# Attention steps split into turn and value products, head pairs side by side, a reordered mixer and a delta-net norm summed by tokens

## The chip, the cores and the metric

The kernel runs on one core of one Trainium2 chip. The metric is the device time of one execution in microseconds (us), as the median of several runs. A core has a matrix engine (TensorE, PE in the rows), a vector engine (VectorE, DVE), a scalar engine (ScalarE, ACT), GpSimd (POOL) and a queue of transfers (SyncE, SP). Each takes its own instructions in order, and they wait for one another through semaphores. Products go into the banks of PSUM, from which VectorE and ScalarE copy them out.

## The reference

Two blocks work on 256 tokens of 1024 features, in float32. The first block has a convolution with a dense MLP, an attention with a forget gate, and a mixture of experts; the second has a mixer and an MLP. The change touches the forget attention and the mixer.

```python
def forgetting_attention(q, k, v, logf_cum):       # 16 heads of 64, causal
    ...
    s = jnp.einsum("bqhd,bkhd->bhqk", qf[:, q0:q1], kf[:, :q1]) * scale
    s = s + logf_cum[:, :, q0:q1, None] - logf_cum[:, :, None, :q1]
    ...
    p = jax.nn.softmax(s, axis=-1).astype(v.dtype)
    outs.append(jnp.einsum("bhqk,bkhd->bqhd", p, v[:, :q1]))

# the mixer: 8 heads of block attention, 8 heads of a gated delta net, on one projection
proj = jnp.einsum('bsd,dc->bsc', h, w_in[l])
o_att = moba_attention(att_q, att_k, att_v, rel_bias)          # 256 tokens: one causal block
o_gdn = gated_deltanet(gdn_qkv, gdn_z, gdn_a, gdn_b, ...)
mix = jnp.einsum('bsc,cd->bsd', jnp.concatenate([o_att, o_gdn], axis=-1), w_out[l])

# the delta net: convolution and SiLU, norm of q and k by heads, decays g, chunks of 64 tokens
g = -jnp.exp(A_log) * jax.nn.softplus(a + dt_bias)
uw = lax.linalg.triangular_solve(a_mat, rhs, left_side=True, lower=True, unit_diagonal=True)
...
o = o * lax.rsqrt(jnp.mean(o * o, axis=-1, keepdims=True) + EPS) * norm_w
o = o * jax.nn.silu(z)
```

## The kernel before

**Products and weights.** A float32 product by weights is made of three products of rounded parts: hi by hi, hi by lo and lo by hi. Each weight block comes by DMA (raw); ScalarE rounds it (whi) and VectorE takes the difference (wlo). A projection chunk is 256 columns wide and consists of 48 matmuls of 256 columns. Products of computed values (scores, value products, the deltanet's) are plain float32, of which each is two instructions in the trace.

**Order.** The program is written as Python that emits instructions; a scheduler sets the order on each engine, and tc.issue_after(x) keeps what follows behind x. last_pe[0] is the last matmul or transpose emitted by mm or transpose, so a block under tc.issue_after(last_pe[0]) stands behind it. In the mixer, seq(...) runs each of its steps in that way; in the forget attention the steps are emitted in the order of a string, without a pin.

**Forget attention (forget_block).** k_chunk, q_chunk and v_chunk project 256 columns each, that is four heads (banks pk, pq, pv). lin_small makes the 16 forget logits (bank psm), which VectorE brings to the buffer smo, two transposes (bank pf) turn, and softplus rows (sp_...) turn into gates; forget_gates sums them over the tokens (bank pc) into nlc, which each head's scores take in as a bias. For a pair of heads, att_scores makes biases and score products (bank sc) and the softmax; its two heads lie on rows 0 to 63 and 64 to 127 of the same operands. att_values transposes the probabilities (bank pt, three for each head), ScalarE copies them (pT), and the value products go to the two halves of the columns of one bank (po). In the string, s stands for the scores of a pair, o for values, and q, k, v for chunks.

**Mixer (mixer_block).** Projections of the block attention (paq for q and k, pav for v) and of the delta net (pqkv, six gdn_chunk; pz, two gate_chunk) stand in one sequence with the pairs of the attention. The delta net's small product gives a and b (psm, smo, transposes pab), from which softplus rows and gg make the decays; five products with a triangle of ones sum them up (pgc). gdn_chunk copies its bank to cpad and makes a convolution of eight rows on VectorE (qkv). After all chunks head_sums (pn) and a root, a reciprocal and a split in two parts (two_parts, buffer parts) give the norms of q and k, which normalize spreads over the heads by products (pbc). Then gdn_scores makes decays and scores for four pairs of heads (pdec, ps), v_tokens turns v (pvt), first_level and level solve the triangular systems by doubling (pi, pu, pm, pog), and out_rows makes pieces of the output projection (acc). At the end the delta net's output is squared (osq), summed by heads (bank pn of 8 rows, in the code pn2), and its norm is spread with two matmuls a bank (pob) and multiplied in, together with the gate zs.

Of the kernel before, what the change touches and what calls it, by code (L numbers as in the profile page):

```python
# [10 lines left out]
AF = mybir.ActivationFunctionType  # L11
# [3 lines left out]
P = 128  # L15
T = 256
# [86 lines left out]
def kernel(ctx: ExitStack, tc: tile.TileContext, ins: dict, out: bass.AP):  # L103
# [749 lines left out]
    def att_values(hp, probs, vtok, ohi, olo):  # L853

        po = bank("po", "acc")
        pTs = []
        for j in range(2):
            pt = bank("pt")
            for i in range(3):
                pe.transpose(pt[:, i * P:(i + 1) * P], probs[j][:, i * P:(i + 1) * P], ident)  # L860
            pT = wk("pT", 384)
            act.activation(pT, pt[:, :384], AF.Copy)
            pTs.append(pT)
        for j in range(2):
            s = slice(j * 64, (j + 1) * 64)
            vc = slice((2 * hp + j) * 64, (2 * hp + j + 1) * 64)
            mm(po[s, 0:T], vtok[0][:, vc], pTs[j][:, 0:T], True, False)
            mm(po[s, P:T], vtok[1][:, vc], pTs[j][:, T:384], False, True)
        split(ohi, olo, po[:, :T])


    def forget_block(x, feed, nxt):
# [16 lines left out]
        def forget_logits():  # L889
            fT = lin_small(ins["w_f"], 16, hkv, feed.R, -1.0)  # L890
# [28 lines left out]

        def values(hp):  # L920
            att_values(hp, pend.pop(hp), vt, oT[0][hp], oT[1][hp])
# [349 lines left out]
    def mixer_block(x, feed, nxt):  # L1271
# [68 lines left out]

        def att_out():
            h_, pr = pend.pop(0)
# [15 lines left out]
        qk_out(1, 0, first[1])  # L1358

# [3 lines left out]
        for tb in range(2):  # L1363
            pe.transpose(pab[:, tb * 16:(tb + 1) * 16], abT[:16, tb * P:(tb + 1) * P], ident[0:16, 0:16])
# [4 lines left out]
        act.activation(v3(beta, 8), pab3[:, :, 8:16], AF.Sigmoid)  # L1369
        gg = sm("gg", 16, bufs=1)  # L1370
# [8 lines left out]
        for tb in range(2):  # L1379
            mm(pg[:, tb * 8:(tb + 1) * 8], C("tri"), gg[:, tb * 8:(tb + 1) * 8], True, True)  # L1380
        mm(pg[:, 16:24], C("ones"), gg[:, 0:8], True, True)
        mm(pg[:8, 256:384], gg[:, 0:8], C("tri"), True, True)
        mm(pg[:8, 384:512], gg[:, 8:16], C("tri"), True, True)
# [23 lines left out]
        seq(lambda: gdn_chunk(4), lambda: gdn_chunk(5))  # L1407
# [3 lines left out]
        seq(head_sums)  # L1411
# [17 lines left out]
        seq(lambda: gate_chunk(0), normalize)  # L1429
# [151 lines left out]
        seq(v_tokens, lambda: gdn_scores(0), lambda: gate_chunk(1))  # L1581
# [276 lines left out]
```

## Time and profile before

| | us |
|---|---|
| Timed runs: median of 3 | 1704.89 (1704.25 to 1707.17) |
| Profiled execution | 1699.43 |
| its span in the trace | 1697.7 |
| TensorE busy in it | 1625.0 (96%) |
| VectorE busy | 1250.7 (74%) |
| ScalarE busy | 1016.9 (60%) |
| GpSimd busy | 78.9 (5%) |

The stages in the trace are: convolution and MLP until 323.5 us, forget attention to 449.1, experts to 1284.1, the mixer to 1503.9 and the last MLP to the end. The mixer's projections and block attention take 1302.9 to 1397.2, the scores of the delta net and its first levels until 1435.4, the later levels until 1485.8, the norm and the last pieces of the output projection until 1503.9. Busy shares are a mean over stages with different limits, so they don't say what a change in one stage is worth; the waits in that stage do.

### The profile page before, as it was taken

The page shows a single profiled execution, that of the slowest core. Times are in us where ns is not written, and L with a number is a line of the kernel's source. Part 1 is how long each engine was busy: PE and PEld are TensorE (multiplying, and loading weights), DVE is VectorE, ACT ScalarE, POOL GpSimd, SP SyncE. Part 2 cuts the span into 40 slices and gives each one's busy share as a digit, 9 for nine tenths or more (in the row PEclk, how much of TensorE's full clock was granted, in tenths as well). Part 3 has the DMA queues.
Part 4 walks back from the last instruction along what each step waited for, and adds up shares of the span by engine and source line. Part 5 has one row for each costly group of instructions (what it writes and reads, how often), then busy time and mean ns, then how long its engine had stood idle before and what let it go on. Part 6 is the DMA issues. An engine that isn't in the chain of part 4 may idle for free.

```text
span 1697.7 us, 26302 instructions
## 1 busy us (share of the span) xinstructions
PE 1625.0 (96%) x10450; PEld 1375.9 (81%) x10450; DVE 1250.7 (74%) x1738; ACT 1016.9 (60%) x1464; POOL 78.9 (5%) x113
## 2 busy tenths in 40 slices
PE   7999999999889999999999999999998988989998
PEld 6769999898778788777878778787777877879997
DVE  4466555676578998989988898989887775385554
ACT  4245444565467777777777777777676454354442
POOL 2400000000000000000000000000000000011111
PEclk9989999999899999999999999999999998999999
DMA  6655555435528889999999998899995341035551
GB/s 237 186 181 192 178 194 177 175 133 199 199 103 324 323 335 355 343 351 352 335 337 352 373 356 335 338 349 341 361 354 186 125 142 46 3 139 200 196 180 45
DMA packets 59973, 408.71 MB, mean 241 GB/s; under 512 B 7353, under 2 KB 7745, under 8 KB 12609
## 3 DMA queue, kind: packets, MB, share of 16 engines
q1 hardware_dynamic: 56448, 396.86, 63.4%
q0 software_dynamic: 3104, 9.55, 2.0%
q8 instruction: 85, 1.39, 0.3%
q10 hardware_dynamic: 288, 0.52, 0.1%
q14 instruction: 48, 0.39, 0.1%
HBM read 404.67 MB, written 2.24 MB: 240 GB/s over the span
## 4 chain that ended last, share of the span: by engine, by line
PE 60%; DVE 5%; ACT 3%; issue 2%; DMA 1%; POOL 0%; DVEq 0%; POOLq 0%; ACTq 0%
PE pgu L145 27%; PE acc L145 18%; PE pu L145 6%; DVE wlo L156 2%; PE pi L145 2%; PE paq L145 1%; ACT whi L167 1%; PE pqkv L145 1%; PE mpt L1178 1%; PE scat L145 1%; DMA raw<-in_moe_w_down_dram 1%; ACT xg L1058 0%; DVE qkv L159 0%; DVE Vi L156 0%; PE po L145 0%
## 5 line engine op out<-in xcount | busy, mean ns | idle before, releaser
L156 DVE TENSOR_TENSOR wlo<-raw,whi 128x1024 fp32r<-128x1024 f32 x752 | 890.8, 1222 | 254.7 <-ACT whi L167 246.8
L167 ACT ACTIVATE whi<-raw 128x1024 fp32r<-128x1024 f32 x752 | 761.1, 1057 | 256.0 <-PE pu L145 71.8
L145 PE MATMUL pgu<-whi,xg 128*128 128x512 f32 x1408 | 467.7, 398 | 5.9 <-DVEq L1106 4.1
L145 PEld LDWEIGHTS pgu<-whi,xg 128*128 128x128 f32 x1408 | 265.6, 189 | 63.2 <-PEq L1106 4.4
L145 PE MATMUL pgu<-wlo,xg 128*128 128x512 f32 x704 | 283.8, 403 | 1.1 <-issue 1.0
L145 PEld LDWEIGHTS pgu<-wlo,xg 128*128 128x128 f32 x704 | 132.9, 189 | 39.6 <-DVE wlo L156 13.2
L145 PE MATMUL acc<-wlo,mhi 128*128 128x512 f32 x352 | 135.1, 391 | 1.1 <-DVE wlo L156 1.1
L145 PE MATMUL acc<-whi,mlo 128*128 128x512 f32 x352 | 134.4, 389 | 0.0
L145 PE MATMUL acc<-whi,mhi 128*128 128x512 f32 x352 | 127.1, 390 | 1.4 <-ACT whi L167 1.4
L145 PE MATMUL pu<-hlo,whi 128*128 128x256 f32 x432 | 122.3, 283 | 0.5 <-DVE hlo L159 0.5
L145 PE MATMUL pu<-hhi,whi 128*128 128x256 f32 x432 | 122.2, 283 | 0.0
L145 PE MATMUL pu<-hhi,wlo 128*128 128x256 f32 x432 | 122.2, 283 | 0.0
L1072 ACT ACTIVATE msg<-pgu,rse 128x256 f32<-128x256 f32 x88 | 41.8, 475 | 81.1 <-PE pgu L145 81.1
L145 PE MATMUL acc<-wlo,fhi 128*128 128x512 f32 x216 | 85.1, 394 | 0.0
L145 PE MATMUL acc<-whi,fhi 128*128 128x512 f32 x216 | 85.0, 394 | 0.0
L145 PE MATMUL acc<-whi,flo 128*128 128x512 f32 x216 | 85.0, 394 | 0.0
L167 ACT ACTIVATE mhi<-mpt 128x256 fp32r<-128x256 f32 x88 | 33.9, 385 | 84.5 <-PE mpt L1178 84.5
L145 PEld LDWEIGHTS pu<-hlo,whi 128*128 128x128 f32 x432 | 82.7, 191 | 1.3 <-DVE hlo L159 0.7
L145 PEld LDWEIGHTS pu<-hhi,whi 128*128 128x128 f32 x432 | 82.6, 191 | 0.6
L145 PEld LDWEIGHTS pu<-hhi,wlo 128*128 128x128 f32 x432 | 82.7, 191 | 0.0
L145 PEld LDWEIGHTS acc<-wlo,mhi 128*128 128x128 f32 x352 | 66.1, 188 | 17.1 <-DVE wlo L156 3.3
L145 PEld LDWEIGHTS acc<-whi,mhi 128*128 128x128 f32 x352 | 65.9, 188 | 15.8 <-ACT whi L167 2.0
(400 smaller groups left out, 2640.8 us busy)
## 6 DMA issues: line engine op xcount, KB each, us to landing
raw<-in_moe_w_gu_dram SPq DMA_DIRECT2D x172, 1024.0 KB, 6.4
raw<-in_moe_w_down_dram SPq DMA_DIRECT2D x86, 1024.0 KB, 6.3
raw<-in_w_up_dram SPq DMA_DIRECT2D x16, 1024.0 KB, 4.8
raw<-in_w_down_dram SPq DMA_DIRECT2D x16, 1024.0 KB, 4.9
raw<-in_w_in_dram SPq DMA_DIRECT2D x14, 1024.0 KB, 4.8
raw<-in_ffn_w_gate_dram SPq DMA_DIRECT2D x11, 1024.0 KB, 4.9
raw<-in_ffn_w_up_dram SPq DMA_DIRECT2D x11, 1024.0 KB, 4.8
raw<-in_ffn_w_down_dram SPq DMA_DIRECT2D x11, 1024.0 KB, 4.8
```

The source lines that it names most:

```text
L145: last_pe[0] = pe.matmul(o, l, r, start=start, stop=stop, skip_group_check=True).ins
L156: return (eng or dve).tensor_tensor(out=o, in0=a, in1=b, op=op)
L167: return act.activation(hi, src, AF.Copy), tt(lo, src, f(hi), ALU.subtract, eng)
L1072: act.activation(sg, pgu[:, 0:256], AF.Silu, scale=r)
L1178: pe.transpose(pt[:, j * P:(j + 1) * P], p["sg"][:, j * P:(j + 1) * P], ident)
```

## The change

The scores of a pair get both banks ahead, and the two heads alternate instruction by instruction. att_values is split: att_turn makes the transposes and copies, att_values the products, with the two heads alternating. In the forget attention the string has a new letter t for the turn, each step is pinned behind the last matmul, the forget logits are transposed after v_chunk(0), and q_chunk(0) comes ahead of the gates. In the mixer the projections, the attention steps, gate_chunk(1), the decay products and the pieces of the output projection take other places. The delta net's norm is summed with the tokens on the partitions (16 small matmuls into a bank of 16 columns), so that root and reciprocal work on 128 by 16 elements, and it is spread with a broadcast as the stationary operand.

```diff
@@ att_scores, att_values
+        pss, rows = [bank("sc") for _ in range(2)], [slice(j * 64, (j + 1) * 64) for j in range(2)]
+        if add_bias:
+            for j in range(2):
+                add_bias(pss[j][:, 0:384], 2 * hp + j)
+        for j, s in enumerate(rows):
+            mm(pss[j][:, 0:P], qT[s, 0:P], kT[s, 0:P], not add_bias, True)
+        for j, s in enumerate(rows):
+            mm(pss[j][:, P:P + T], qT[s, P:T], kT[s, :], not add_bias, True)
         for j in range(2):
             h = 2 * hp + j
-            s = slice(j * 64, (j + 1) * 64)
-            ps_ = bank("sc")
-            if add_bias:
-                add_bias(ps_[:, 0:384], h)
-            mm(ps_[:, 0:P], qT[s, 0:P], kT[s, 0:P], not add_bias, True)
-            mm(ps_[:, P:P + T], qT[s, P:T], kT[s, :], not add_bias, True)
+            ps_ = pss[j]
...
+    def att_values(hp, pTs, vtok, ohi, olo):
+
+        po = bank("po", "acc")
+        for w in range(2):
+            for j in range(2):
+                s = slice(j * 64, (j + 1) * 64)
+                vc = slice((2 * hp + j) * 64, (2 * hp + j + 1) * 64)
+                mm(po[s, w * P:T], vtok[w][:, vc], pTs[j][:, w * T:T + w * P], w == 0, w == 1)
         split(ohi, olo, po[:, :T])
@@ forget_block
         k_chunk(0)
-        nls = forget_logits()
+        small = lin_small_mm(ins["w_f"], 16, hkv, feed.R, -1.0)
         v_chunk(0)
+        nls = forget_logits(small)
         feed.rest()
         k_chunk(1)
+        q_chunk(0)
         forget_gates(nls)
-        for step in "q0 s0 s1 q1 o0 v1 o1 s2 s3 k2 o2 q2 o3 v2 s4 s5 k3 o4 q3 o5 s6 s7 v3 o6 o7".split():
-            {"k": k_chunk, "q": q_chunk, "v": v_chunk, "s": scores, "o": values}[step[0]](int(step[1]))
+        steps = {"k": k_chunk, "q": q_chunk, "v": v_chunk, "s": scores, "t": turn, "o": values}
+        for step in ("v1 s0 s1 q1 t0 k2 o0 t1 s2 q2 o1 t2 s3 v2 o2 t3 s4 k3 o3 t4 s5 q3 o4 t5 s6 s7 v3 o5 t6 t7 o6 o7"
+                     .split()):
+            with tc.issue_after(last_pe[0]):
+                steps[step[0]](int(step[1]))
@@ mixer_block
+        seq(lambda: gdn_chunk(2))
+        x = feed.base()
...
+        seq(lambda: att_probs(0))
         gg = sm("gg", 16, bufs=1)
...
-        seq(lambda: gdn_chunk(2), lambda: att_probs(0), lambda: v_chunk(0))
-        x = feed.base()
+        seq(lambda: v_chunk(0), lambda: att_probs(1), lambda: gdn_chunk(3))
...
+        seq(decays)
...
-        seq(lambda: att_probs(1), lambda: gdn_chunk(3), att_out, lambda: qk_chunk(0, 1), att_out, lambda: qk_chunk(1, 1),
-            lambda: att_probs(2), lambda: gdn_chunk(0), lambda: att_probs(3), lambda: v_chunk(1), att_out,
-            lambda: gdn_chunk(1), att_out)
+        seq(att_t, lambda: qk_chunk(0, 1), att_out, att_t, lambda: qk_chunk(1, 1), att_out, lambda: gdn_chunk(0),
+            lambda: att_probs(2), lambda: gdn_chunk(1), lambda: att_probs(3), lambda: v_chunk(1), att_t)
...
-        seq(lambda: gdn_chunk(4), lambda: gdn_chunk(5))
+        seq(lambda: gdn_chunk(4), att_out, att_t, lambda: gdn_chunk(5))
...
-        seq(head_sums)
+        seq(att_out, head_sums)
...
-        seq(lambda: gate_chunk(0), normalize)
+        seq(lambda: gate_chunk(0), lambda: gate_chunk(1), normalize)
...
-        seq(v_tokens, lambda: gdn_scores(0), lambda: gate_chunk(1))
-        seq(lambda: gdn_scores(1), lambda: out_rows(0, 0), lambda: first_level(0), lambda: out_rows(1, 0),
-            lambda: gdn_scores(2), lambda: level(0, 2), lambda: out_rows(2, 0), lambda: gdn_scores(3))
+        seq(lambda: gdn_scores(0), v_tokens, lambda: out_rows(0, 0), lambda: gdn_scores(1), lambda: out_rows(1, 0),
+            lambda: out_rows(2, 0), lambda: first_level(0), lambda: gdn_scores(2), lambda: level(0, 2),
+            lambda: out_rows(3, 0), lambda: gdn_scores(3))
...
-        seq(lambda: out_rows(3, 0), lambda: level(0, 4), lambda: first_level(1))
+        seq(lambda: level(0, 4), lambda: first_level(1))
...
         def out_sums():
-            for b in range(4):
-                mm(pn2[:8, :T], v3(C("ind"), 16)[:, b, 0:8], osq[:, b * T:(b + 1) * T], b == 0, b == 3)
+            for tb in range(2):
+                for b in range(4):
+                    mm(pn2[:, tb * 8 + 2 * b:tb * 8 + 2 * b + 2], osq[:, b * T + tb * P:b * T + (tb + 1) * P],
+                       v3(C("ind"), 16)[:, 0, 0:2], True, True)
...
-        rn2 = two_parts(rn2, 8)
...
             for b in range(4):
-                mm(pbs[b // 2][:, b % 2 * T:(b % 2 + 1) * T], hsel[0:40, b * P:(b + 1) * P], rn2, True, True)
+                for tb in range(2):
+                    o = b % 2 * T + tb * P
+                    for j in range(2):
+                        c = tb * 8 + 2 * b + j
+                        mm(pbs[b // 2][j * 64:(j + 1) * 64, o:o + P], rn2[:, c:c + 1].to_broadcast([P, 64]), ident, True, True)
```

How the instructions stand now is shown at three places. First TensorE in the forget attention, at the first pair's value products before. Its six transposes and three pv matmuls stand just ahead of these rows, and v_chunk(1), whose matmuls 4 to 7 are the pv rows, goes on behind po.

```order
L145 MATMUL pv_3698<-whi_3701,hhi_3119 128x256
L145 MATMUL pv_3698<-wlo_3702,hhi_3119 128x256
L145 MATMUL pv_3698<-whi_3701,hlo_3121 128x256
L145 MATMUL po_3679<-pT_3684,v_3198 64x256
L145 MATMUL po_3679<-pT_3684,v_3199 64x128
L145 MATMUL po_3679<-pT_3690,v_3198 64x256
L145 MATMUL po_3679<-pT_3690,v_3199 64x128
L145 MATMUL pv_3698<-whi_3701,hhi_3119 128x256
```

And after the change: the end of a k chunk, the value products of pair 0, the turn of pair 1 and the scores of pair 2.

```order
L145 MATMUL pk_3752<-hhi_3120,wlo_3760 128x256
L145 MATMUL po_3812<-pT_3744,v_3198 64x256
L145 MATMUL po_3812<-pT_3750,v_3198 64x256
L145 MATMUL po_3812<-pT_3744,v_3199 64x128
L145 MATMUL po_3812<-pT_3750,v_3199 64x128
L148 MATMUL pt_3819<-cm,sc_3658 128x128 x3
L148 MATMUL pt_3825<-cm,sc_3669 128x128 x3
L145 MATMUL sc_3831<-nlc_3211,rsel 128x384
L145 MATMUL sc_3832<-nlc_3211,rsel 128x384
L145 MATMUL sc_3831<-kT_3200,qT_3202 128x128
L145 MATMUL sc_3832<-kT_3200,qT_3202 128x128
L145 MATMUL sc_3831<-kT_3200,qT_3202 128x256
```

The chunk between turn and products is whole now, and the rows of two heads alternate in po and sc. Second, TensorE in the mixer at the decay products: before, they stand behind v_chunk(0) and ahead of the scores of pair 1.

```order
L145 MATMUL pav_13192<-whi_13199,hhi_12809 128x256
L145 MATMUL pav_13192<-wlo_13200,hhi_12809 128x256
L145 MATMUL pav_13192<-whi_13199,hlo_12811 128x256
L145 MATMUL pgc_13255<-gg_13067,cm 128x8 x3
L145 MATMUL pgc_13255<-cm,gg_13067 8x128 x2
L145 MATMUL sc_13269<-ak_12881,aq_12880 128x128
L145 MATMUL sc_13269<-ak_12881,aq_12880 128x256
L145 MATMUL sc_13283<-ak_12881,aq_12880 128x128
L145 MATMUL sc_13283<-ak_12881,aq_12880 128x256
```

After the change they stand directly behind the last three matmuls of gdn_chunk(3).

```order
L145 MATMUL pqkv_13283<-hhi_12809,whi_13290 128x256
L145 MATMUL pqkv_13283<-hlo_12811,whi_13290 128x256
L145 MATMUL pqkv_13283<-hhi_12809,wlo_13291 128x256
L145 MATMUL pgc_13353<-gg_13167,cm 128x8 x3
L145 MATMUL pgc_13353<-cm,gg_13167 8x128 x2
L148 MATMUL pt_13367<-cm,sc_13145 128x128 x3
L148 MATMUL pt_13373<-cm,sc_13156 128x128 x3
L145 MATMUL paq_13379<-hhi_12808,whi_13382 128x256
```

So between them and the chunk whose bank VectorE has to copy out there is nothing on TensorE any more. Third, VectorE at the same place: before, the rows of gg (which the decay products read) stand among the convolution rows of gdn_chunk(2).

```order
L159 SCALAR_TENSOR_TENSOR sp_acc_13078<-sp_acc_13078,sp_z_13072 128x16
L159 SCALAR_TENSOR_TENSOR qkv_12877<-cpad_13153,cm,qkv_12877 128x256
L159 SCALAR_TENSOR_TENSOR gg_13067<-sp_acc_13078,sp_m_13088 128x16
L159 SCALAR_TENSOR_TENSOR qkv_12877<-cpad_13153,cm,qkv_12877 128x256
L159 SCALAR_TENSOR_TENSOR gg_13067<-gg_13067,ea_13091 128x16
```

After the change, behind the copy cpad of gdn_chunk(3) come the last softplus sum, a weight split, and gg.

```order
L156 TENSOR_TENSOR cpad_13342<-pqkv_13283,R_13052 128x2x256
L159 SCALAR_TENSOR_TENSOR sp_acc_13178<-sp_acc_13178,sp_z_13172 128x16
L156 TENSOR_TENSOR wlo_13529<-raw_13526,whi_13528 128x1024
L159 SCALAR_TENSOR_TENSOR gg_13167<-sp_acc_13178,sp_m_13188 128x16
L163 TENSOR_SCALAR qkv_12877<-cpad_13342,cm 128x256
L159 SCALAR_TENSOR_TENSOR gg_13167<-gg_13167,ea_13191 128x16
```

The last row that writes gg has moved behind the copy of gdn_chunk(3).

## Rows read from the trace of the kernel before

**Rows 1.** Windows: us, busy us by engine (PE, PEld, DVE, ACT, POOL), clock, DMA.
```profile
353.40:429.50 76.10, 73.88 (x582) 66.38 (x581) 48.77 (x159) 43.04 (x110) 0.00 (x0) 1.00 0.53 196
449.10:1284.10 835.00, 817.95 (x3674) 651.95 (x3672) 738.56 (x833) 614.27 (x790) 7.32 (x12) 0.99 0.88 327
...
1302.90:1397.20 94.30, 82.86 (x645) 75.89 (x645) 67.25 (x176) 50.15 (x90) 2.13 (x6) 0.98 0.38 137
1397.20:1435.40 38.20, 33.46 (x354) 28.17 (x354) 21.73 (x42) 14.06 (x34) 0.00 (x0) 0.87 0.16 56
```

**Rows 2.** Groups by line, TensorE, forget attention: busy us, mean ns | idle before, releaser.
```profile
L145 PE MATMUL pk<-hlo,whi 128*128 128x256 f32 x64 | 18.2, 284 | 0.7 <-DVE hlo L159 0.7
...
L145 PE MATMUL po<-pT,v 128*64 128x256 f32 (+1 forms) x64 | 10.1, 339 | 1.1 <-ACT pT L862 1.0
L145 PE MATMUL sc<-kT,qT 64*128 64x128 f32 (+1 forms) x64 | 8.3, 328 | 1.1 <-DVE qT L156 1.1
...
L893 PE MATMUL pf<-cm,smo 16*128 16x16 f32 x2 | 0.3, 219 | 1.3 <-DVE smo L159 1.3
```

**Rows 3.** Groups by line, TensorE, mixer from 1284 to 1435.4 us.
```profile
L145 PE MATMUL po<-pT,av 128*64 128x256 f32 (+1 forms) x32 | 5.0, 339 | 4.0 <-ACT pT L862 4.0
...
L145 PE MATMUL sc<-ak,aq 64*128 64x128 f32 (+1 forms) x32 | 3.7, 350 | 1.5 <-DVE ak L156 1.5
...
L145 PE MATMUL pbc<-parts,hsel 48*128 48x256 f32 x8 | 1.2, 288 | 3.4 <-DVE parts L156 3.4
...
L1364 PE MATMUL pab<-cm,smo 16*128 16x16 f32 x2 | 0.3, 204 | 2.3 <-DVE smo L159 2.3
```

**Rows 4.** Windows of the trace, three stretches of the mixer at a lower granted clock.
```profile
1306.93:1310.34 3.41, 3.41 (x18) 3.41 (x18) 0.95 (x5) 1.20 (x2) 0.00 (x0) 0.50 0.60 250
...
1399.09:1402.50 3.41, 3.41 (x16) 3.08 (x18) 2.04 (x4) 1.20 (x2) 0.00 (x0) 0.50 0.84 303
1416.16:1422.98 6.82, 6.02 (x45) 4.81 (x47) 1.42 (x4) 0.77 (x2) 0.00 (x0) 0.50 0.05 22
```

**Rows 5.** Timeline of TensorE around the first po: start, us, instructions.
```profile
363.87 0.28 PE L145 MATMUL pv<-wlo,hhi 128*128 128x256 f32 x1
363.99 0.28 PE L145 MATMUL pv<-whi,hlo 128*128 128x256 f32 x1
364.32 1.24 PE L145 MATMUL po<-pT,v 128*64 128x256 f32 x8
365.49 0.39 PE L145 MATMUL pv<-whi,hhi 128*128 128x256 f32 x1
```

**Rows 6.** Timeline of TensorE in the deltanet's end.
```profile
1477.83 1.97 PE L145 MATMUL pog<-N,gu 128*64 128x128 f32 x32
...
1486.07 1.89 PE L145 MATMUL pn<-osq,cm 128*8 128x256 f32 x8
...
1491.35 0.71 PE L145 MATMUL pob<-parts,hsel 40*128 40x256 f32 x4 [1.79 <-DVE parts L156]
```

**Rows 7.** Timeline of TensorE: the first scores, and two pairs of scores later.
```profile
353.39 0.61 PE L145 MATMUL sc<-nlc,rsel 64*128 64x384 f32 x3
...
356.88 0.39 PE L145 MATMUL pq<-hhi,whi 128*128 128x256 f32 x1
...
396.81 0.44 PE L145 MATMUL sc<-nlc,rsel 64*128 64x384 f32 x1
...
398.95 0.39 PE L145 MATMUL pk<-hhi,whi 128*128 128x256 f32 x1
```

**Rows 8.** Groups by form, VectorE, mixer: the reciprocals of two shapes.
```profile
L1670 DVE RECIPROCAL rn<-rn 8x256 f32<-8x256 f32 x1 | 1.7, 1742 | 0.8 <-ACT rn L1669 0.8
...
L549 DVE RECIPROCAL sp_z<-sp_z 128x16 f32<-128x16 f32 x1 | 0.3, 253 | 0.0
```

**Rows 9.** Timeline of VectorE behind a gdn_chunk of the mixer.
```profile
1328.06 0.69 DVE L156 TENSOR_TENSOR cpad<-pqkv,R 128x512 f32<-128x512 f32 x1 [0.18 <-PE pqkv L145]
1328.66 1.22 DVE L156 TENSOR_TENSOR wlo<-raw,whi 128x1024 fp32r<-128x1024 f32 x1
```

More of the change, by code (lines that the diff above doesn't have):

```diff
@@ L851, in att_scores, with att_turn @@
         return res
-    def att_values(hp, probs, vtok, ohi, olo):
-        po = bank("po", "acc")
+    def att_turn(probs):
         pTs = []
@@ L859, in att_values @@
             for i in range(3):
-                pe.transpose(pt[:, i * P:(i + 1) * P], probs[j][:, i * P:(i + 1) * P], ident)
+                transpose(pt[:, i * P:(i + 1) * P], probs[j][:, i * P:(i + 1) * P])
             pT = wk("pT", 384)
@@ L863, in att_values @@
             pTs.append(pT)
[L864 to L868, printed above, removed]
+        return pTs
+    def att_values(hp, pTs, vtok, ohi, olo):
[5 more added lines that the diff above has]
+                mm(po[s, w * P:T], vtok[w][:, vc], pTs[j][:, w * T:T + w * P], w == 0, w == 1)
         split(ohi, olo, po[:, :T])
@@ L887, in forget_block, with forget_logits @@
         pend = {}
-        def forget_logits():
-            fT = lin_small(ins["w_f"], 16, hkv, feed.R, -1.0)
+        def forget_logits(small):
+            fT = lin_small_out(*small)
             pf = bank("pf")
@@ L918, in add_bias, with turn @@
             mm(o, row_sel()[s, h:h + 1].to_broadcast([64, P]), nlc[s], True, False)
+        def turn(hp):
+            pend[hp] = att_turn(pend[hp])
         def values(hp):
@@ L1339, in att_probs, with att_t @@
             pend.append((hp, att_scores(hp, aq[:, hp * T:(hp + 1) * T], ak[:, hp * T:(hp + 1) * T], None, mask_of)))
+        turned = []
+        def att_t():
+            h_, pr = pend.pop(0)
+            turned.append((h_, att_turn(pr)))
         def att_out():
-            h_, pr = pend.pop(0)
+            h_, pr = turned.pop(0)
             o = slice(h_ * T, (h_ + 1) * T)
@@ L1362, in mixer_block @@
         pab = bank("pab")
-        for tb in range(2):
-            pe.transpose(pab[:, tb * 16:(tb + 1) * 16], abT[:16, tb * P:(tb + 1) * P], ident[0:16, 0:16])
+        with tc.issue_after(last_pe[0]):
+            for tb in range(2):
+                last_pe[0] = pe.transpose(pab[:, tb * 16:(tb + 1) * 16], abT[:16, tb * P:(tb + 1) * P],
+                                          ident[0:16, 0:16]).ins
         ya = sm("ya", 16, bufs=1)
@@ L1374, in mixer_block, with decays @@
         stt(v3(gg, 8), v3(gg, 8), -1.0, ea[:, None, :].to_broadcast([P, 2, 8]), ALU.mult, ALU.mult)
-        seq(lambda: gdn_chunk(2), lambda: att_probs(0), lambda: v_chunk(0))
-        x = feed.base()
+        seq(lambda: v_chunk(0), lambda: att_probs(1), lambda: gdn_chunk(3))
         pg = bank("pgc")
[L1379 to L1383, printed above, removed]
+        def decays():
+            for tb in range(2):
+                mm(pg[:, tb * 8:(tb + 1) * 8], C("tri"), gg[:, tb * 8:(tb + 1) * 8], True, True)
+            mm(pg[:, 16:24], C("ones"), gg[:, 0:8], True, True)
+            mm(pg[:8, 256:384], gg[:, 0:8], C("tri"), True, True)
+            mm(pg[:8, 384:512], gg[:, 8:16], C("tri"), True, True)
+        seq(decays)
         ngc = sm("ngc", 16, bufs=1)
@@ L1662, in out_sums @@
         def out_sums():
-            for b in range(4):
-                mm(pn2[:8, :T], v3(C("ind"), 16)[:, b, 0:8], osq[:, b * T:(b + 1) * T], b == 0, b == 3)
+            for tb in range(2):
+                for b in range(4):
+                    mm(pn2[:, tb * 8 + 2 * b:tb * 8 + 2 * b + 2], osq[:, b * T + tb * P:b * T + (tb + 1) * P],
+                       v3(C("ind"), 16)[:, 0, 0:2], True, True)
         seq(out_sums, lambda: out_rows(3, 1))
-        rn2 = wk("rn2", T, rows=8)
+        rn2 = sm("rn2", 16, bufs=1)
         with tc.issue_after(ready.ins):
-            act.activation(rn2, pn2[:8, :T], AF.Sqrt, scale=1.0 / 64, bias=C("eps")[:8])
+            act.activation(rn2, pn2[:, :16], AF.Sqrt, scale=1.0 / 64, bias=C("eps"))
         dve.reciprocal(out=rn2, in_=rn2)
-        rn2 = two_parts(rn2, 8)
         nwc = V("gdn_norm_w_2", 0)
@@ L1679, in spread @@
             for b in range(4):
-                mm(pbs[b // 2][:, b % 2 * T:(b % 2 + 1) * T], hsel[0:40, b * P:(b + 1) * P], rn2, True, True)
+                for tb in range(2):
+                    o = b % 2 * T + tb * P
+                    for j in range(2):
+                        c = tb * 8 + 2 * b + j
+                        mm(pbs[b // 2][j * 64:(j + 1) * 64, o:o + P], rn2[:, c:c + 1].to_broadcast([P, 64]), ident, True, True)
         seq(spread)
```

## The prediction

> **What bounds the kernel now.** I read the table by stretches first. TensorE is busy 818 of the 835 us of the expert stage, which the change does not touch, and 73.9 of 76.1 us in the main part of the forget attention; the mixer's stretch with projections and block attention leaves it idle 11.4 us of 94.3 and the deltanet scores 4.7 of 38.2 [rows 1]. VectorE is busy 48.8 and 67.3 us in the two attention stretches. So TensorE sets the pace wherever the change acts, and there are two ways to gain: its waits, and the time its own instructions take. The groups by line name the waits: in the forget stage 1.3 us for pf, 1.1 for sc, 1.1 for po, 0.7 for hlo [rows 2]; in the mixer 2.3 for pab, 4.0 for po, 1.5 for sc, 3.4 for pbc [rows 3]. The clock is the third thing: after the waits of 2.31 and 3.40 us stand stretches of 3.41 us at a granted clock of 0.50, the lower of the two levels (1.2 GHz), and in the first levels another of 6.82 us [rows 4].
>
> **Forget attention.** (a) *Pairs in time.* The po products of a pair start at 364.32 and the next chunk follows at 365.49: 1.17 us for four products of 256 and four of 128 columns, 12 units of 128 [rows 5]. The nearest row in which column halves already alternate is pog, 32 instructions of 128 columns in 1.97 us, some 0.06 each [rows 6]; 12 of those are 0.74 us. That is 0.43 us a pair, 3.4 us for eight pairs. The bounds are nothing (the halves already overlap) and 4.0. Scores: two pairs in a row take 396.81 to 398.95, 2.14 us, and the first two 353.39 to 356.88, which without the 1.1 us for qT is 2.4 [rows 2, 7]; that is 1.07 and 1.20 for a pair. The products of a pair are 12 units of 128 columns too, 0.74 us as pog, and its two biases of 384 columns come on top, 0.18 to 0.35 by the 0.12 us for 256 columns of a projection. I take 0.95 with the row halves alternating, against 1.24 as the pairs with a chunk between them start up anew: 0.29 a pair, 2.3 us; bounds 0.8 (1.05 against 1.15) and 3.5 (0.8 against 1.24).
> (b) *Unbroken chunks.* Four projection chunks are cut by a po after six matmuls. The last pv starts at 363.99, po at 364.32: 0.33 us where two pv stand 0.12 apart, and the resumed pv follows po with its own start-up [rows 5]. I take 0.25 a cut, 1.0 us; bounds 0.4 and 1.6.
> (c) *Waits.* q_chunk(0) now lies ahead of the gates and v1 between them and the first scores, so qT has a chunk (5.9 us, 48 matmuls 0.12 apart) to be ready: 1.08 us goes. Every pT but the last ones has a chunk between its transposes and its products: of the 1.1 us of po waits all goes, but the tail "t6 t7 o6 o7" has only the other pair's transposes (0.8 us) as cover where the copies took it 1.0 us longer on the mean of four [rows 3]; I leave 0.4 there. pf no longer waits: 1.3 us; but the softplus rows now stand on VectorE between the hlo rows for which pk already waits 0.7 us [rows 2], and I give 0.85 back.
> The sum: 3.4 + 2.3 + 1.0 + 1.1 + 0.7 + 0.45 = 9.0 us less; 5 to 11 by the bounds. A step (chunk, scores, turn, products) is some 8 us, of which VectorE works 0.64, its share of the stretch [rows 1], so the softmax of a pair has time before its turn.
>
> **Mixer, projections and block attention.** gdn_chunk(2) moves ahead of the pab transposes and hides smo: the 2.3 us wait goes; with it, I take it, the 3.41 us at half clock behind it, which lost 1.7. Its weights stand ready: in the trace before it starts with no wait of its own behind pab. The turn moves a chunk ahead of each product but the last: 4.0 us of po. Scores of the second half get two chunks of cover behind qk(1,1): 1.5 us. Two gate chunks instead of one stand between the head sums and pbc; the root, its reciprocal and the parts behind it need 3.4 us more than one gate gives [rows 3], and the second gives 5.9: 3.4 us. Side by side: four po pairs at 0.43 and four score pairs at 0.13 (they have no bias): 2.2. In all 15.1.
> What it adds: the decay products pgc now stand on TensorE directly behind gdn_chunk(3), and the order of VectorE puts the copy of that same chunk out of PSUM (cpad), a weight split (wlo) and two softplus rows ahead of the gg they read. The nearest rows: cpad starts 0.18 us after its chunk and occupies 0.60 to the next start, the split some 1.2 [rows 9]; with the last sums, one convolution row and gg itself about 1.0 more. I take 3.0 us, behind which all projections queue, since TensorE takes its instructions in order. The bounds are 0.5 (gg is already done, if VectorE's real order differs) and 3.4. As behind the pab wait of 2.31 us I add a stretch at half clock, 1.7 us. So 15.1 - 4.7 = 10.4 less; bounds 5 and 15.
>
> **Deltanet scores and first levels.** The second gate chunk (5.9 us) leaves its place between scores 0 and 1, and v_tokens with twelve output products comes in, with more output products ahead of the first level. Against me: the scores' copies on VectorE and ScalarE have less cover. For me: two blocks of output products now stand ahead of the first level, whose N is one of these copies. The waits of this stretch are 4.7 us by its busy time [rows 1]; if the order hid 3.9 of them and two further stretches of 3.41 us came at half clock (1.7 each) [rows 4], it is 0.5 less. I take that; the bounds are 3 more and 6 less (waits hidden and half the present slow stretches gone).
>
> **Norm by tokens.** Before, TensorE waits 1.79 us for parts ahead of pob [rows 6], most of it a reciprocal on eight rows by 256 elements of 1.74 us, where one on 128 rows by 16 elements took 0.25 [rows 8], and the two-part split falls away, so the six output products behind the sums (1.6 us) cover root and reciprocal: 1.8 us goes. The sums become 16 instructions of two columns: between 16 times 0.06 and twice the 1.89 of pn's eight; I take 1.9, no change. The spread becomes 32 instructions of 128 columns, 1.9 us by the pog row, instead of 0.71; but the multiplication behind it starts after the first bank, so 0.3 to 1.2 comes back. Net 1.0 less; bounds 1.8 less and 0.5 more.
>
> **Sum.** 9.0 + 10.4 + 0.5 + 1.0 = 20.9 us. The profiled execution of 1699.43 us (span 1697.7) would become 1678.5. The median of the timed runs, 1704.89, is 5.5 above the profiled one; the change is the same there: 1684.0 us. What cannot be told from no change in this kernel is about 0.2%, 3.4 us.
>
> **Rivals.**
> *1. Copies out of PSUM become the bound.* TensorE shortens each pair by 0.7 us, but the softmax rows on VectorE and the pT copies on ScalarE do not shorten. For it: VectorE is busy 0.64 and 0.71 of the two attention stretches already, the mixer's pT copies held four products up by 4.0 us [rows 3], and every chunk's weights are split on the same two engines. Against it: chunks of 5.9 us lie between. If the side-by-side gain (3.4 + 2.3 + 2.2) turns into waits and half of the removed po and sc waits come back elsewhere (3.8), 9.2 us are left: some 1695.5 us (1691 to 1700). The Trainium skill, TensorEngine Tiling (Array Packing), section PSUM Bottleneck, speaks for this case: it says that tiling speeds up TensorE but not the evacuation of PSUM, which may then be what limits. The VectorE shares above are as yet under one, so I hold this less likely than the forecast.
> *2. Side by side does nothing*, since the instructions of the two heads already overlap as far as they can: four heads in 2.14 us is less than their instructions' sum. Without 3.4 + 2.3 + 2.2 the sum is 13.0: 1692 us.
> *3. No change to be measured*: 1 and 2 together with the bad bounds of pgc, deltanet and norm; within 1701.5 to 1708.3.
> *4. Slower: the half clock lasts.* The second gate chunk was the dense work between the first two score blocks. If without it TensorE stays at the lower level from pbc to the end of the first levels, the 33.5 busy us of that stretch, about 29 at full clock (0.87 mean), take 58: 25 us more, which brings 1709. It decides from 24 us of full-speed work done at the lower level. For it: 0.87 is the lowest clock of the four stretches [rows 1], and the drops sit just there. Against: the first drop follows an idle time of 3.40 us that goes, and output products are dense.
>
> **Chances.** Forecast 0.65, its own range 1678 to 1691. Rival 1 0.18, rival 2 0.08, rival 3 0.04, rival 4 0.05. Leaving out the worst of rival 1, rivals 3 and 4 and the best tail, 1675 to 1696 holds eight in ten. Faster by over 0.2% in the first three cases, 0.91; the same 0.04; slower 0.05.
>
> **What would show it.** In the profile after: no waits for pf, qT, pab and only small ones for po; po pairs near 0.74 us and score pairs near 0.95 from first start to the next chunk; a wait of pgc on gg of 3 us just behind gdn_chunk(3), with a stretch at 0.50 behind it; no wait of pbc; pob without its 1.8 us. The forecast is wrong if new waits on VectorE or ScalarE stand behind the transposes or the scores (rival 1), if pairs keep 1.17 and 1.24 us (rival 2), or if the mean clock from pbc on falls far below 0.87 (rival 4).

## The result

| | before | after |
|---|---|---|
| Timed runs, median | 1705.36 (1704.25 to 1707.17, 4 runs) | 1685.61 (1683.75 to 1687.67, 4 runs) |
| Ratio | | 0.9889, 95% interval 0.9873 to 0.9904 |
| Span of the profiled execution | 1697.7 | 1683.9 |
| TensorE busy in it | 1625.0 | 1623.7 |

The medians differ by 19.75 us, where 20.9 was forecast; 1684.0 was forecast for the time. The two spans differ by only 13.8, which the first experiment explains. TensorE's busy time is nearly the same in these two traces, so what differs there is idle time, 12.5 us of it.

The windows of the trace after the change, in the columns of [rows 1], for the stretches that answer to it: first scores to last value products of the forget attention, experts, mixer from the row statistics to pbc, and pbc to the products with Y of the first long level (at 1435.39 before, at 1420.57 after).

```profile
359.77:422.65 62.88, 62.44 (x529) 55.78 (x528) 45.85 (x156) 41.34 (x108) 0.00 (x0) 1.00 0.51 184
443.21:1278.52 835.31, 819.22 (x3674) 653.33 (x3672) 738.52 (x833) 613.77 (x790) 7.32 (x12) 0.99 0.88 327
1296.78:1389.98 93.20, 88.91 (x698) 81.94 (x696) 67.92 (x177) 51.31 (x92) 1.91 (x6) 0.96 0.41 144
1389.98:1420.57 30.59, 25.77 (x306) 21.07 (x305) 20.38 (x41) 12.88 (x33) 0.00 (x0) 0.94 0.17 63
```

In the forget attention TensorE is idle 0.44 us of 62.9, where it was 2.2 of 76.1 [rows 1] (5.9 us of the difference in length is v1, which now lies ahead of the first scores). In the mixer it is still idle 4.3 us of 93.2, with a second gate chunk inside. Behind pbc it is idle 4.8 us of 30.6 (0.55 of it a new wait for zs), where it was 4.7 of 38.2 with that gate chunk inside: there the new order hid next to none of the waits. Which waits these are is told by the groups by line, first those of the forget attention, the same groups as [rows 2]:

```profile
L145 PE MATMUL pk<-hlo,whi 128*128 128x256 f32 x64 | 18.2, 284 | 0.7 <-DVE hlo L159 0.7
...
L145 PE MATMUL pq<-hlo,whi 128*128 128x256 f32 x64 | 18.3, 286 | 0.5 <-DVE hlo L159 0.5
...
L145 PE MATMUL po<-pT,v 128*64 128x256 f32 (+1 forms) x64 | 7.2, 339 | 0.3 <-ACT pT L864 0.3
...
L145 PE MATMUL sc<-kT,qT 64*128 64x128 f32 (+1 forms) x64 | 6.7, 323 | 0.0
...
L900 PE MATMUL pf<-cm,smo 16*128 16x16 f32 x2 | 0.3, 219 | 0.0
```

The waits for pf and qT are gone, that for pT fell from 1.1 to 0.3. hlo now holds up pq as well, by 0.5 us. The groups of the mixer, which answer to [rows 3], with those that are new:

```profile
L145 PE MATMUL po<-pT,av 128*64 128x256 f32 (+1 forms) x32 | 3.5, 339 | 0.0
...
L145 PE MATMUL sc<-ak,aq 64*128 64x128 f32 (+1 forms) x32 | 3.7, 350 | 0.0
...
L145 PE MATMUL pqkv<-hhi,whi 128*128 128x256 f32 x96 | 27.7, 289 | 1.2 <-ACT R L444 1.2
...
L145 PE MATMUL pav<-whi,hhi 128*128 128x256 f32 x32 | 9.3, 289 | 0.4 <-DVE cpad L156 0.4
...
L145 PE MATMUL pgc<-gg,cm 128*128 128x8 f32 x6 | 1.3, 336 | 2.7 <-DVE gg L159 2.7
...
L145 PE MATMUL pbc<-parts,hsel 48*128 48x256 f32 x8 | 1.5, 303 | 0.6 <-DVE zs L156 0.6
...
L1388 PE MATMUL pab<-cm,smo 16*128 16x16 f32 x2 | 0.3, 218 | 0.0
```

The waits for pT (4.0), ak (1.5), smo (2.3) and parts (3.4) are gone. In their place stand 2.7 us for gg, 1.2 for R, 0.4 for cpad and 0.6 for zs: 11.2 us of waits went and 4.9 came.

### The profile page after: what moved, and what is told of

Read it like the earlier page. It is cut to its first block, busy times and chain, and to the rows that moved or that the text cites. A ratio compares the mean times of both kernels' runs of the same rounds, so it can differ in the third digit from the quotient of the medians.

```text
span 1683.9 us, 26370 instructions
## 1 busy us (share of the span) xinstructions
PE 1623.7 (96%) x10486; PEld 1377.5 (82%) x10486; DVE 1246.5 (74%) x1737; ACT 1016.2 (60%) x1463; POOL 77.8 (5%) x112
```

## Where the time went, stage by stage

The table has the time between the first instructions of some groups in the timelines of TensorE: two profiled executions of the kernel before (the second is from the first experiment) and two after (the second from the ninth).

| from, to | before | before, second | after | after, second |
|---|---|---|---|---|
| first k chunk, first transposes of the experts | 125.63 | 125.66 | 118.54 | 118.53 |
| experts, to the mixer's first product | 834.99 | 836.72 | 835.31 | 837.58 |
| rb, head sums | 81.88 | 81.92 | 77.95 | 76.44 |
| head sums, last level (pm) | 91.78 | 93.85 | 87.76 | 85.32 |
| output sums, first transposes of the MLP | 17.79 | 19.11 | 16.59 | 16.61 |

So the forget attention gave 7.1 us, the projections and block attention 3.9 to 5.5, the scores and levels with the wait of pbc 4.0 to 8.5, and the norm 1.2 to 2.5. Most of the spread inside a kernel is the clock's. The stretch from the head sums to the last level shows it; before, then after:

```profile
1384.23:1476.00 91.77, 80.32 (x1415) 69.79 (x1415) 47.91 (x96) 36.21 (x80) 0.39 (x1) 0.94 0.13 48
...
1374.73:1462.49 87.76, 79.65 (x1416) 69.89 (x1415) 48.17 (x97) 35.79 (x81) 0.00 (x0) 0.96 0.15 57
```

TensorE is idle 11.5 us there before and 8.1 after, and the second traces show nearly the same, 11.8 and 8.2. The waits thus gave 3.3 to 3.5 us in both pairs of traces. The remainder is busy time, which follows the granted clock: 10.2 and 13.7 us at 0.50 stood in this stretch in the two traces before, 6.8 and none in the two after.

The same holds for the whole. On the third chip the mean granted clock of the runs is 0.9836 before (11 runs) and 0.9864 after (5 runs). By their mean spans, 1701.3 and 1681.6 us, the missing share of the clock comes to 27.8 and 22.9 us. So of the 19.7 us between these spans some 5 us, by this estimate, is time at half clock, and some 15 is waits and work.

## Experiments

The kernel before ran beside them: 1704.54 in the median on the first chip, 1704.04 on the second, 1702.43 on the third. Each is told against that of its chip.

### The kernel before, once more

No edit.

> The kernel before, unchanged, for a second profile and a second set of times. The first profiled execution took 1699.43 us, its timed runs 1704 to 1707, while the profiled execution after the change lies among its timed runs; so the two spans differ by 13.8 us and the medians by 19.75. Theory A: the first profile caught an execution with fewer or shorter stretches at the lower clock, and the change is worth about 20; then a second profile lies some 3 to 6 us higher and the additional time stands in stretches at a granted clock of 0.50. Theory B: profiled executions of this kernel are always some 5 us shorter than timed ones; then the span comes out at 1697 to 1699 again.

Measured: median 1704.59 of ten runs, ratio 0.9996 (0.9984 to 1.0008), and a profiled execution of 1706.94 with a span of 1705.2. The mean granted clock over the span is 0.982, where the first profile had 0.985; the missing share of the span is 30.7 us against 25.5, time lost at the lower level: 5.2 of the 7.5 us between the spans. The rest stands ahead of the first k chunk, which starts at 325.96 us here and at 323.46 in the first trace, with 10.2 us at the lower level ahead of it in both. Windows of the second trace, in two places where the first had less:

```profile
457.41:471.06 13.65, 9.83 (x45) 9.64 (x45) 6.95 (x32) 4.66 (x11) 1.08 (x2) 0.50 0.22 79
...
1498.48:1501.89 3.41, 2.85 (x7) 2.28 (x8) 3.41 (x9) 3.32 (x6) 0.00 (x0) 0.50 0.00 0
```

The first stands at the start of the experts, where the first profile had 10.24 us at this level in place of 13.65; the second behind the wait of pob, where it had none. A third, 3.41 us from 1478.00, was not in the first profile either. Theory A holds: the first profile was a favoured execution, and the change is worth what the medians say. A single pair of spans is no measure of 14 against 20 us here.

### The two heads in the old order, in the kernel after

```diff
         res = []
-        pss, rows = [bank("sc") for _ in range(2)], [slice(j * 64, (j + 1) * 64) for j in range(2)]
...
+        for j in range(2):
+            h = 2 * hp + j
+            s = slice(j * 64, (j + 1) * 64)
+            ps_ = bank("sc")
...
-        for w in range(2):
-            for j in range(2):
+        for j in range(2):
+            for w in range(2):
```

> The kernel after the change, but with the instructions of the two heads in the old order: bias and products of one head, then of the other, in scores and value products. The forecast's theory, side by side saves TensorE time: the time comes back as in its terms, 3.4 for the forget value products, 2.3 for the scores, 2.2 in the mixer, and by the two traces (1.17 to 0.80 us a pair of value products, twelve pairs, 0.2 for each forget score pair) some 5 to 6 us slower than after, about 1691. The rival, TensorE overlaps the two heads in any order: same as after within 2 us.

Measured: median 1686.02, ratio 0.9881 (0.9850 to 0.9911), which is not to be told from after. The timeline of TensorE, at the first lone pair: value products, turn, scores, next chunk.

```profile
373.30 0.88 PE L145 MATMUL po<-pT,v 128*64 128x256 f32 x8
374.10 0.87 PE L148 MATMUL pt<-cm,sc 128*128 128x128 f32 x6
374.91 0.44 PE L145 MATMUL sc<-nlc,rsel 64*128 64x384 f32 x1
...
376.22 0.39 PE L145 MATMUL pq<-hhi,whi 128*128 128x256 f32 x1
```

And the same place in the kernel after:

```profile
374.16 0.87 PE L145 MATMUL po<-pT,v 128*64 128x256 f32 x8
374.96 0.88 PE L148 MATMUL pt<-cm,sc 128*128 128x128 f32 x6
375.76 0.44 PE L145 MATMUL sc<-nlc,rsel 64*128 64x384 f32 x2
376.04 0.82 PE L145 MATMUL sc<-kT,qT 64*128 64x128 f32 x8
376.79 0.39 PE L145 MATMUL pq<-hhi,whi 128*128 128x256 f32 x1
```

The value products of a pair take 0.80 us from their start to the turn in both orders. Only the scores differ: 1.31 us against 1.03. From the first scores to the experts this kernel takes 84.81 us and the one after 83.44: in this order of the steps, side by side is worth 1.4 us in the forget attention, not the 5.7 of its two terms there.

### Alternating alone, in the kernel before

```diff
@@ in the kernel before: att_scores and the products of att_values as after, turn and products together
+        pss, rows = [bank("sc") for _ in range(2)], [slice(j * 64, (j + 1) * 64) for j in range(2)]
...
-        for j in range(2):
+        for w in range(2):
+            for j in range(2):
```

> The kernel before with one part of the change alone: the instructions of the two heads alternate in scores and value products, and nothing moves. The forecast's terms for it are 3.4 + 2.3 + 2.2 = 7.9 us, so 1696.7. The theory from the run of the changed kernel in the old order within pairs (there the value products of a pair took 0.80 us in either order, and only the forget scores of a pair differed, by 0.28): what stretched a pair of value products to 1.17 us before is that the second head's copy of the turned probabilities ends 0.37 us after the first, which alternating does not change; so 1 to 2 us faster, from the forget scores alone.

Measured: median 1703.25, ratio 0.9995 (0.9981 to 1.0009): no change to be measured. The forecast's term of 7.9 us fails here, and the 1 to 2 us expected from the scores are not seen either: the forget attention takes 125.46 us, against 125.63 and 125.66. The timeline keeps 1.17 us for a lone pair of value products: the first starts at 367.23 and the next chunk at 368.40.

### The forget attention alone, and the mixer alone

```diff
@@ forget attention alone: shared functions and forget_block as after; in the mixer as before, with
+            att_values(h_, att_turn(pr), [av[:, 0:512], av[:, 512:1024]], ohi[0][:, o], olo[0][:, o])
@@ mixer alone: shared functions, mixer and norm as after; in forget_block as before, with
+            att_values(hp, att_turn(pend.pop(hp)), vt, oT[0][hp], oT[1][hp])
```

> The changed forget attention and the shared score and value functions side by side, with the mixer's old order (turn directly ahead of the products) and the old norm. By the traces the forget stage is worth 7.1 us and the mixer's pairs 1.5: 8 to 9 us faster than before, about 1696.5. If the forecast's 9.0 for forget alone were right, 10 to 11 faster. The rival, that the gain comes from the mixer alone and forget gives its time back in the stage behind it: 0 to 3 us faster.

> The changed mixer, norm and shared functions, with the forget attention in its old order (turn directly ahead of the value products). If the two halves add up, this is the change of 20 less the 8.7 to 11 that the changed forget attention gave alone: 9 to 12 us faster than before, some 1694. By the forecast's terms it would be 11.9 and the pairs in forget on top. The rival, that the halves are not independent (the forget stage's new end shifts when weights arrive): under 7 or over 14.

Measured: forget alone 1693.18, ratio 0.9949 (0.9930 to 0.9968), 5 to 12 us faster; mixer alone 1692.84, ratio 0.9925 (0.9902 to 0.9948), 9 to 17 us faster. 8.7 by the ratio and 12.8 by the ratio make 21.5, the whole change within its interval: the halves add up, and the forecast's split of 9.0 and 11.9 is inside both, which are wide. Inside the mixer the single moves were not run apart; what each gave is read from the waits that went. In the first kernel the forget stage takes 118.5 us, as after, and the mixer keeps its old times. That mixer has alternating heads and a turn directly ahead of the products:

```profile
1319.62 0.82 PE L148 MATMUL pt<-cm,sc 128*128 128x128 f32 x6
1321.20 1.24 PE L145 MATMUL po<-pT,av 128*64 128x256 f32 x8 [0.76 <-ACT pT L864]
1322.37 0.39 PE L145 MATMUL paq<-hhi,whi 128*128 128x256 f32 x1
```

Here a pair takes 1.17 us again, from 1321.20 to 1322.37. So it is not the order of the heads but the distance of the turn that decides. ScalarE copies the two heads' turned probabilities one after the other (timeline of ScalarE in the kernel before, at the first po of [rows 5]):

```profile
363.80 0.84 ACT L862 ACTIVATE pT<-pt 128x384 f32<-128x384 f32 x2
```

Two copies in 0.84 us, the second started 0.37 after the first. Among the single products of the trace, the first of the first head starts at 364.32 and that of the second at 364.70, 0.37 us later and 0.05 behind the end of its copy; by [rows 5] the pair is 0.37 longer than 0.80. When a chunk lies between, both copies are done, and TensorE works on both halves of the columns at once in either order.

### The decay products one chunk later

```diff
-        seq(decays)
...
-        seq(att_t, lambda: qk_chunk(0, 1), att_out, att_t, lambda: qk_chunk(1, 1), att_out, lambda: gdn_chunk(0),
+        seq(att_t, lambda: qk_chunk(0, 1), att_out)
+        pg = bank("pgc")
+        seq(decays)
...
+        seq(att_t, lambda: qk_chunk(1, 1), att_out, lambda: gdn_chunk(0),
```

> The kernel after the change, with the five decay products moved from behind gdn_chunk(3) to behind the first value products of the mixer, one projection chunk later. The forecast's theory: the 2.7 us wait on gg goes, and with it the stretch at the lower clock behind it, which by the trace cost the decay products, a turn and a chunk 3.3 us: 6 us faster than after, about 1680. The rival, that the clock falls there anyhow or that another wait takes the place (the copies of the chunk come before the sums of gg on VectorE all the same): 0 to 3 us faster.

The place in the kernel after, on VectorE and then on TensorE:

```profile
1319.20 0.68 DVE L156 TENSOR_TENSOR cpad<-pqkv,R 128x512 f32<-128x512 f32 x1
1319.80 0.16 DVE L159 SCALAR_TENSOR_TENSOR sp_acc<-sp_acc,sp_z 128x16 f32<-128x16 f32 x1
1319.89 1.22 DVE L156 TENSOR_TENSOR wlo<-raw,whi 128x1024 fp32r<-128x1024 f32 x1
...
1321.37 0.17 DVE L159 SCALAR_TENSOR_TENSOR gg<-gg,ea 128x16 f32<-128x16 f32 x1
```

```profile
1321.59 1.28 PE L145 MATMUL pgc<-gg,cm 128*128 128x8 f32 x6 [2.69 <-DVE gg L159]
...
1323.76 1.54 PE L148 MATMUL pt<-cm,sc 128*128 128x128 f32 x6
1324.95 0.56 PE L145 MATMUL paq<-hhi,whi 128*128 128x256 f32 x1
```

VectorE copies the bank of gdn_chunk(3), makes a softplus sum, splits a weight for 1.2 us, and only then comes the last row of gg; pgc starts 0.05 us behind that row's end, after 2.69 us. Behind it a turn of six takes 1.19 us to the next chunk, where it takes 0.57 to 0.63 elsewhere in this stage, and the chunk's first matmuls stand 0.21 apart: the granted clock is 0.50 from 1321.8 for 6.83 us. In the experiment:

```profile
1323.38 0.87 PE L145 MATMUL po<-pT,av 128*64 128x256 f32 x8
1324.18 0.84 PE L145 MATMUL pgc<-gg,cm 128*128 128x8 f32 x6
...
1325.48 0.87 PE L148 MATMUL pt<-cm,sc 128*128 128x128 f32 x6
1326.11 0.36 PE L145 MATMUL paq<-hhi,whi 128*128 128x256 f32 x1
```

No wait, the turn takes 0.63, and from rb to the head sums it is 72.01 us against 77.95. Median 1678.75, ratio 0.9861 (0.9838 to 0.9883), where the kernel after had 0.9889 and, on the third chip, 0.9884. The wait and the clock behind it were worth 5.9 us against that trace and 4.4 against the second one after (76.44). Nine traces have the changed mixer. In the six with the wait for gg a stretch of 3.41 or 6.83 us at 0.50 starts within 2 us of the wait's end; the three without it (this one and two below) have none there. So the theory holds: the wait took the clock down.

### The bank of the row statistics

```diff
-                    self.bc["ps"] = bank("rb")
+                    self.bc["ps"] = bank("rb", "acc") if getattr(self, "rb_acc", False) else bank("rb")
```

The flag is set in the mixer alone, and the decay products stand one chunk later, as in the experiment above.

> The kernel with the decay products one chunk later (the run before it in this study: 1678.75), and the mixer's row-statistics product (rb) in a bank of the other ring of PSUM, so that gdn_chunk(2) need not wait until ScalarE has read rb. In the trace after the change gdn_chunk(2) waits 1.18 us for that. If the wait is by the bank alone: 1.2 us faster than that run, some 1677.5. The rival: the next bank of the ring is free no sooner (the copies of the first two chunks wait for the same statistics): no difference.

Measured: median 1677.62, ratio 0.9847 (0.9816 to 0.9879). The timeline of TensorE, first in the kernel after, then in this one:

```profile
1296.78 0.60 PE L145 MATMUL rb<-cm,rr 128*128 128x128 f32 x4
1298.57 0.39 PE L145 MATMUL pqkv<-hhi,whi 128*128 128x256 f32 x1 [1.18 <-ACT R L444]
...
1294.34 0.60 PE L145 MATMUL rb<-cm,rr 128*128 128x128 f32 x4
1294.70 0.36 PE L145 MATMUL pqkv<-hhi,whi 128*128 128x256 f32 x1
```

gdn_chunk(2) starts 0.36 us after rb with no wait, where after the change it waited 1.18 us for R; rb to the head sums takes 70.62 us against 72.01. The wait was by the bank. In the time of the whole the 1.1 us lies inside the intervals.

### The gate chunk back between the scores

```diff
-        seq(lambda: gate_chunk(0), lambda: gate_chunk(1), normalize)
+        seq(lambda: gate_chunk(0), normalize)
-        seq(lambda: gdn_scores(0), v_tokens, lambda: out_rows(0, 0), lambda: gdn_scores(1), lambda: out_rows(1, 0),
+        seq(lambda: gdn_scores(0), lambda: gate_chunk(1), v_tokens, lambda: out_rows(0, 0), lambda: gdn_scores(1), lambda: out_rows(1, 0),
```

> The kernel after the change, with gate_chunk(1) back behind the first scores, ahead of v_tokens. The forecast's theory: pbc waits again, 3.4 us, and by the other terms of that stretch nothing else moves: some 3 us slower than after, 1689. The rival: the gate's 5.9 dense us give the score copies cover and hold the clock up, so the waits behind them (0.6, 0.4 and 1.2 us in the first levels) shrink and a stretch at 0.50 goes: the same as after or 1 to 2 us faster.

Measured: median 1683.22, ratio 0.9888 (0.9851 to 0.9924), the same as after; the 3 us expected by the forecast's theory did not come. The wait comes back, but smaller:

```profile
1382.45 1.18 PE L145 MATMUL pbc<-parts,hsel 48*128 48x256 f32 x8 [1.32 <-DVE parts L156]
```

1.32 us in place of 3.40 [rows 3]; and from the head sums to pm it takes 86.67 us, between the two traces after (87.76 and 85.32). So moving the gate bought nothing that can be told: most of the 3.4 us had gone already with the other moves. The chain to the parts begins with the copy of the last chunk on VectorE; before, and here:

```profile
1385.23 0.69 DVE L156 TENSOR_TENSOR cpad<-pqkv,R 128x512 f32<-128x512 f32 x1
...
1371.01 0.69 DVE L156 TENSOR_TENSOR cpad<-pqkv,R 128x512 f32<-128x512 f32 x1
```

The head sums start at 1384.23 and 1371.56, so the copy comes 1.00 us behind their start before and 0.55 ahead of it here. For 0.80 of this a pair of value products now stands between the last chunk and the head sums; for the rest, a weight split holds the copy up for less time. From the copy to the end of the parts it is another 0.5 us less. That makes the 2.1 us by which the wait shrank; these moves were not run apart.

### Three kernels side by side

> The kernel after the change, unchanged, timed on one chip beside the three others of this call. If the forecast's sum of 20.9 us holds: 1683 to 1686, 18 to 21 less than before. If the first median was favoured by its chip: under 16 less.

> The decay products one chunk later, rb in a bank of the other ring, and gate_chunk(1) back behind the first scores. With the gate back the trace showed a wait of pbc of 1.3 us in place of 3.4 before, and 1.1 us less from the head sums to the last levels, with one stretch at 0.50 less. If that was the order, this is 1 us faster than the run without the gate back (1677.6), some 1676.5; if it was only where the stretches at 0.50 fell, the same within 1 us or 1 slower.

> The kernel after the change with the old norm of the delta net (sums by heads on eight rows, root and reciprocal on 8 by 256, split in two parts, four spreading products). The forecast's term: 1.0 slower than after. By the traces the stretch from the sums to the end of the output projection took 17.8 us in the first profile before and 19.1 in the second, where a stretch at 0.50 stood behind the wait, and 16.6 after: so 1.2 to 2.5 slower than after. The rival, that the 32 spreading instructions cost what the reciprocal saved: the same within 0.5.

The edits are none; the three edits above in one kernel; and the sums, the split and the spread of the norm as before in the kernel after.

| on the third chip | median | ratio to before |
|---|---|---|
| after, once more | 1683.12 | 0.9884 (0.9864 to 0.9904) |
| decays late, bank, gate back | 1676.35 | 0.9848 (0.9830 to 0.9867) |
| after with the old norm | 1687.34 | 0.9899 (0.9882 to 0.9917) |

The change is 19.3 us on this chip too. The second kernel is the fastest of the study and beats the changed one by 6.8 us in the medians; whether the gate's place has a part in it can't be told (1677.62 without it). The old norm costs 4.2 us in the medians and 2.6 by the ratios, whose intervals overlap by more than half. By the mean spans and granted clocks of the two (1684.8 at 0.9852, 1681.6 at 0.9864) some 2 us of it is time at half clock and some 1 us the rest. Its trace shows the wait and what comes behind it:

```profile
1476.51 0.71 PE L145 MATMUL pob<-parts,hsel 40*128 40x256 f32 x4 [1.79 <-DVE parts L156]
1478.01 0.80 PE L145 MATMUL acc<-whi,ohi 128*128 128x512 f32 x1 [0.79 <-ACT ohi L167]
```

```profile
1477.24:1484.07 6.83, 6.07 (x14) 4.79 (x15) 5.12 (x10) 3.32 (x6) 0.00 (x0) 0.50 0.10 18
```

The wait of 1.79 us for parts is back, and TensorE is granted 0.50 for 6.83 us behind it. The stretch from the sums to the MLP takes 20.63 us there, against 16.61. In the kernel after it reads:

```profile
1472.50 2.02 PE L145 MATMUL pn<-cm,osq 128*128 128x2 f32 x16
...
1475.94 1.97 PE L145 MATMUL pob<-cm,rn 128*64 128x128 f32 x32
1478.07 0.50 PE L145 MATMUL acc<-whi,ohi 128*128 128x512 f32 x1 [0.16 <-ACT ohi L167]
```

The sums take 1.88 us to the next product, the spread 1.97, and nothing waits but 0.16 us.

## Why the prediction was right, and where its terms were off

- **The whole.** 20.9 us were forecast, 19.75 and 19.3 measured. The time came out right in part by luck, since two large errors cancel. The terms for waits and work add up to 24.3 us, and the third chip shows some 15 by the estimate above. The terms for the clock add up to 3.4 us more lost at half clock, and the third chip shows some 5 less. The waits that were to go and the place of the new one were right, as told below. Rivals 3 and 4 didn't come; the mean clock from pbc to the same products of the levels is 0.94, not below 0.87.
- **Side by side**, 7.9 us in all: the term failed as a cause. Alternating is worth 1.4 us in the forget attention (scores alone, 0.28 a lone pair) and nothing in the mixer, whose lone pairs of scores take 0.86 us in both kernels. As far as rival 2 says that the order of the heads does little, it was right. But its time of 1692 was not reached, because the 0.37 us a pair of the 0.43 that were forecast for the alternation came from the split instead: both copies were ready. By the groups by line the value products fell from 10.1 to 7.2 us in the forget attention and from 5.0 to 3.5 in the mixer, 2.9 and 1.5 us where 3.4 and 1.7 were forecast: the size was nearly right by luck, with another cause. The row at 364.32 [rows 5] shows no idle time, since the first head's products cover the second's wait; I took a wait for work.
- **Rival 1** shows in two small waits (cpad 0.4 us, zs 0.6) and did not bind: VectorE is busy 0.73 of both attention stretches after, and the turn's copies hold up only the tail, by 0.3 us where 0.4 was left.
- **Forget waits.** pf and qT went as forecast; pq's new 0.5 us on hlo is of the 0.85 that was given back. What was left out is the turn between value products and scores, at five places, which takes 0.80 us where one between two chunks takes 0.57. A lone pair of scores takes 1.03 us, not 0.95. The stage gave 7.1 of 9.0 us.
- **Projections and block attention**, without pbc 7.0 forecast: 3.9 and 5.5. The wait of pgc came where and as forecast, 2.7 for 3.0 us; the clock behind it was low for 6.83 us in the one trace (3.4 us lost) and 3.41 in the other (1.7, as forecast). The stretch at half clock behind pab went with its wait. Missed was that gdn_chunk(2), moved ahead, takes the bank that rb leaves, 1.2 us, and that pairs of scores without a bias gain nothing, 0.5.
- **pbc and deltanet**, 3.9 forecast: 4.0 to 8.5. The size is luck. The forecast had 3.4 us of the wait for pbc go, 3.9 of the first levels' waits hidden, and two more stretches at half clock against it. Of the wait 2.9 us went, and most of it not by gate_chunk(1): without its move it is 1.3 us, not 3.4. Of the first levels' waits next to none went: 4.7 us idle before, 4.3 after without the wait for zs. And instead of more time at half clock there was less: 10.2 and 13.7 us of it became 6.8 and none, and half of the difference, 1.7 and 6.8 us, is in the gain.
- **Norm**, 1.0 forecast: 1.2 by the first traces, 2.6 by the ratios of the old norm. The waits and instructions came as forecast; the difference is the clock, since in four of the five traces with the old norm a stretch at half clock stands behind the wait, which the first profile did not have. With the new norm none stands there in eight traces, but in three of them one of 3.41 us comes at the start of the MLP.

## What to carry to other kernels

Where products need a copy of something that the same engine has just made, put a whole chunk between: it hides not only the wait that the profile names, but also the one of the second half, which hides in the duration of the first. A product that is moved to directly behind a chunk queues behind that chunk's own copy on the other engine; one chunk later it costs nothing. And take two profiles of the same kernel before reading small differences from spans.

## What the runs showed of the hardware

TensorE ran the value products of two heads on two halves of its columns at once, 0.80 us a pair, though the program had both products of the one head ahead of those of the other; alternating them changed nothing. Executions of the unchanged kernel lay between 1698.82 and 1710.03 us, and between its two traces 5.2 of 7.5 us is time at 0.50 of the clock: idle times of 1.8 to 3.4 us are followed by 0, 3.41 or 6.83 us of it in different executions. So a wait in these traces cost up to 3.4 us (half of 6.83) more than its row says, and a change that takes waits away is worth more, and varies more, than the sum of the rows.
